# Dilated queries and keys as 2x2 block products: seven products for eight, in a written order

## The chip, the cores and the metric

The kernel runs on one core of one Trainium2 chip. A core has a matrix engine (PE; its weight loads are listed apart, as PEld), three engines for elementwise work (DVE, ACT, POOL), a queue that issues the DMAs (SP) and 16 DMA engines. SBUF holds the working data, PSUM (8 banks of 128 x 512 float32) takes the results of PE. Every engine runs its own instructions in order; semaphores join them. The metric is the device time of one execution in microseconds; lower is better.

## What is computed

One layer of an encoder trunk over 1024 tokens of width 1024, all in float32:

```
h = rmsnorm(x, attn_norm_g)
proj = h @ w_in                      # 1024 x 8096, cut into
# c_q 256 | c_kv 128 | k_rope 32 | z_mla 512 | q_dil 1536 | k_dil 1536 | v_dil 1536 | z_dil 512 | g_mla, g_dil 1024 each
a_out = mla_attention(c_q, c_kv, k_rope, ...)          # 8 heads, dense
d_out = dilated_mixture(q_dil, k_dil, v_dil, positions) # 3 groups of 8 heads of 64
y_mla = (a_out * silu(z_mla)) @ w_o_mla
y_dil = (d_out * silu(z_dil)) @ w_o_dil
merged = sigmoid(g_mla + b) * y_mla + sigmoid(g_dil + b') * y_dil
out = rmsnorm(x + merged @ w_out, final_norm_g)

def dilated_mixture(q, k, v, positions):
    q, k = rope(q heads, positions), rope(k heads, positions)
    for g, (window, dilation) in enumerate(((128, 1), (512, 4), (2048, 16))):
        o, lse = dilated_group(q[g], k[g], v[g], dilation, window // (2 * dilation))
    return sum over g of softmax(lse over g) * o
```

The change is in `q_dil` and `k_dil`: h (1024 x 1024) times 3072 columns of `w_in`, then the rotation by position.

## The kernel before

A float32 product is made of three: each operand is split into a high part `h` (rounded to the matrix engine's fp32r format) and a low part `l`, and `mm3` (line 67) adds h*h, h*l and l*h in one PSUM bank. `split` (line 73) writes the high part with ACT and the low part with the engine it is given. A `w_h`, `w_l` or `hT_h`, `hT_l` in the profile is such a pair.

The stages, in order of the program:

1. `latent_proj` reads x transposed (`xt`), scales it by the norm's gain and keeps it split in SBUF as `hTh`, `hTl` (8 pieces of 128 features x 1024 tokens). The factor of each token (the norm's rsqrt) is applied later, as `R` or `rcol`. `tables` makes cosines and sines, `latents` the queries, keys and values of the dense attention, `dil_v` (line 335) the dilated values, in six calls of 256 columns. Products go to the pool `pj_a` of six PSUM banks; `latents` has a pool of two (`pj_l`).
2. `dil_qk` (line 371) runs twelve times: two halves of the heads (`quad`) x three groups x q and k. One run, an "item", loads two weight tiles of 1024 x 128 (`wtile`, line 79): the first halves of four heads and their second halves, so that the rotation mixes the two results elementwise. For each half of the tokens (512) it makes the two products (`proj_half`: 8 pieces x 3 matmuls each), then `rope` (line 227): four products on DVE, read from PSUM, and two sums on POOL. The result is split (groups 0 and 1; ACT and POOL) or copied (group 2; ACT) into `dq_st`, group 1 and 2 in the order of their dilation, and after both halves it is stored per head to the tensors `s_dq`, `s_dk` in DRAM (line 404).
3. `dil_attention` goes over four pairs of heads and three groups. `dil_head` (line 610) loads q, k and v of one head into `op_b`, `op_a`, `op_c` and works in four steps: scores into `s_ps` (line 634), mask and maximum on DVE with the table `masks` (`soft_block`), exp on ACT, transposes (642), products with v (655, 663). `dil_classes` does group 2. PE's waits are filled by `fillers`: the projections of z and of the gates, pulled a few matmuls at a time by `feed`, one PSUM bank (`pj_b`); nineteen steps of three matmuls (`FIRST_FEED`) stand ahead of the attention.
4. `mla_attention` and then `output`.

The order of the instructions on each engine is not written out: a scheduler goes through the program with a model of the times and issues what is ready, earlier program lines first. Tiles live in pools stacked from the left and the right end of SBUF; a tile of a later pool waits until the tiles that had its place are done. All DMAs are issued by SP (line 65).

Of the kernel before, what the change touches and what calls it, by code (L numbers as in the profile page):

```python
# [39 lines left out]


# [8 lines left out]
class Net:  # L50
# [16 lines left out]
    def mm3(self, out, lh, ll, rh, rl, start, stop):  # L67
        mm = self.nc.tensor.matmul
        mm(out, lh, rh, start=start, stop=False)  # L69
        mm(out, lh, rl, start=False, stop=False)  # L70
        return mm(out, ll, rh, start=False, stop=stop)  # L71
# [7 lines left out]
    def wtile(self, src, wp=None, n=8):  # L79
        raw = self.wp.tile([128, 8, 128], F32, name="w_raw")  # L80
        wp = wp or self.wp
        h = wp.tile([128, 8, 128], F32R, name="w_h")
        l = wp.tile([128, 8, 128], F32R, name="w_l")
# [4 lines left out]
    def proj_half(self, w, half, pool):  # L88

        return run_all(self.proj_steps(w, half, pool))  # L90

    def proj_steps(self, w, half, pool):
# [3 lines left out]
        for kc in range(8):  # L96
            self.mm3(ps, w[0][:, kc], w[1][:, kc], self.hTh[:, kc, t], self.hTl[:, kc, t], kc == 0, kc == 7)
            if kc < 7:
                yield
# [235 lines left out]
    def dil_v(self, g, quad, tp, pj):  # L335
# [3 lines left out]
        for kk in range(2):  # L339
            raw = self.wp.tile([128, 4, 256], F32, name="w_raw")  # L340
            wp = (self.wp, self.wpx)[kk]
            h = wp.tile([128, 4, 256], F32R, name="w_h")
            l = wp.tile([128, 4, 256], F32R, name="w_l")
            self.dma(raw, a["wv"][g * 2 + quad, kk])
            self.split(raw, h, l, nc.gpsimd)
            w.append((h, l))
        for t in range(8):
            ps = pj.tile([128, 512], F32, name="pj")[:, :256]
            for kc in range(8):
                wh, wl = w[kc // 4]  # L350
                sl = slice(128 * t, 128 * t + 128)
                self.mm3(ps, self.hTh[:, kc, sl], self.hTl[:, kc, sl], wh[:, kc % 4], wl[:, kc % 4], kc == 0, kc == 7)
# [18 lines left out]
    def dil_qk(self, g, quad, which, tp, pj):  # L371

        nc, a = self.nc, self.a
        base = T_QK + (g * 2 + quad) * 4 + which * 2
        wa, wb = self.wtile(a["wt"][base]), self.wtile(a["wt"][base + 1], wp=self.wpx)
        if g < 2:
            st = [[tp.tile([128, S], F32R, name=f"dq_st{c}{p}") for p in range(2)] for c in range(2)]
        else:
            st = [[tp.tile([128, S], F32, name=f"dq_st{c}0")] for c in range(2)]
        for half in range(2):  # L380
            c512 = slice(half * 512, half * 512 + 512)
            pa, pb = self.proj_half(wa, half, pj), self.proj_half(wb, half, pj)
            o = self.rope(pa, pb, self.cos_d[:, c512], self.sin_d[:, c512], tp)
            for c in range(2):
                if g == 0:
                    self.split(o[c], st[c][0][:, c512], st[c][1][:, c512], nc.gpsimd)
                    continue
                if g == 1:
                    src = o[c].rearrange("p (m r) -> p r m", r=4)
                    dst = [x.rearrange("p (r m) -> p r m", r=4)[:, :, 128 * half:128 * half + 128] for x in st[c]]  # L390
                    self.split(src, dst[0], dst[1], nc.gpsimd)
                else:

                    src = o[c].rearrange("p (m b e) -> p e b m", b=8, e=2)
                    dst = st[c][0].rearrange("p (e b m) -> p e b m", e=2, b=8)[:, :, :, 32 * half:32 * half + 32]
                    for e in range(2):
                        nc.scalar.copy(out=dst[:, e], in_=src[:, e])
        off = 64 if (g == 0 and which) else 0
        dst = (self.dq if which == 0 else self.dk)[g]
        for c in range(2):  # L400
# [619 lines left out]
```

## Time and profile before

| | us |
|---|---|
| runs of the kernel before | 1333.44, 1323.28, 1328.5; median 1328.5 |
| the profiled execution | 1329.38 |
| its span, first to last instruction | 1327.2 |
| mean granted PE clock | 0.983 |

The profile is one execution. A row of a group gives the line, engine, operation, what it writes and reads, shapes and count, then busy time, mean ns of one, and the idle time of the engine ahead of it with what ended it. A row of a timeline begins with start and duration in us. A row of windows gives busy time (and instructions) of PE, PEld, DVE, ACT and POOL in a stretch of the span, then the granted clock of PE, the share of the DMA engines and GB/s. `L69`, `L70`, `L71` are the three matmuls of `mm3`, wherever it is called from. Starts of matmuls are measured and their ends are modelled, so the distance of starts is what one costs.

The span in 40 slices of 33.2 us (digits are tenths of a slice):

```profile
PE   8999999999999999988989899999999999999998
DVE  7463520222222224656576565656555566559622
ACT  6533332223322335545455463455554555444322
POOL 2251212676467644525422040312111022135522
PEclk9899999999999999989999999999999999999999
```

The stage of `dil_qk` is the stretch of slices 8 to 15 in which DVE shows 2.

### The profile page before, as it was taken

What the parts mean: (1) busy time and instruction counts of PE and PEld (TensorE: products, weight loads), DVE (VectorE), ACT (ScalarE), POOL (GpSimd) and SP (SyncE); (2) the same over time, 40 slices, a digit from 0 to 9 for tenths busy, and PEclk for the clock granted to TensorE, in tenths of its full rate; (3) what the DMA queues carried; (4) which work ended last, traced back from release to release, by engine and by line L of the source; (5) the groups of instructions that cost most, each with busy time, mean ns of one, the idle gap of its engine ahead of it and who ended that gap; (6) DMA issues with size and microseconds to landing.
All of it is one profiled execution on the core that took longest, in us unless ns stands there. A gap on an engine that the chain in (4) does not pass through costs nothing.

```text
span 1327.2 us, 19295 instructions
## 1 busy us (share of the span) xinstructions
PE 1272.2 (96%) x7101; PEld 1106.5 (83%) x7101; DVE 647.8 (49%) x1204; ACT 563.5 (42%) x1102; POOL 455.3 (34%) x302
## 2 busy tenths in 40 slices
PE   8999999999999999988989899999999999999998
PEld 8898999888888887877878777788888888887786
DVE  7463520222222224656576565656555566559622
ACT  6533332223322335545455463455554555444322
POOL 2251212676467644525422040312111022135522
PEclk9899999999999999989999999999999999999999
DMA  9757563575345435678777788636333463136322
GB/s 321 225 163 295 194 238 111 144 212 153 112 110 155 134 111 155 159 188 223 192 186 209 200 211 189 173 106 160 95 92 108 104 178 121 61 123 210 128 93 77
DMA packets 128254, 213.04 MB, mean 161 GB/s; under 512 B 36440, under 2 KB 65696, under 8 KB 126304
## 3 DMA queue, kind: packets, MB, share of 16 engines
q1 hardware_dynamic: 128160, 211.81, 55.2%
q8 instruction: 56, 0.92, 0.3%
q14 instruction: 38, 0.31, 0.1%
HBM read 143.01 MB, written 68.75 MB: 160 GB/s over the span
## 4 chain that ended last, share of the span: by engine, by line
PE 69%; DMA 9%; DVE 6%; issue 2%; SPq 1%; ACT 1%; POOL 0%; DVEq 0%; ACTq 0%; POOLq 0%
PE pj L69 17%; PE pj L71 16%; PE pj L70 16%; PE pt L543 4%; PE av L551 2%; PE av L552 2%; PE s_mla L69 2%; PE s_mla L70 2%; PE s_mla L71 2%; DMA s_sd<-av_t 2%; PE pt L642 1%; PE av L663 1%; SPq L65 1%; PE s_ps L698 1%; PE s_ps L634 1%
## 5 line engine op out<-in xcount | busy, mean ns | idle before, releaser
L76 POOL TENSOR_TENSOR w_l<-w_raw,w_h 128x1024 fp32r<-128x1024 f32 (+1 forms) x70 | 167.5, 2396 | 440.3 <-ACT w_h L75 390.3
L69 PE MATMUL pj<-hT_h,w_h 128*128 128x512 f32 x768 | 314.5, 410 | 2.2 <-DVE zg_z L428 2.1
L71 PE MATMUL pj<-hT_h,w_l 128*128 128x512 f32 x768 | 301.9, 393 | 0.0
L70 PE MATMUL pj<-hT_l,w_h 128*128 128x512 f32 x768 | 301.2, 392 | 0.0
L233 DVE TENSOR_TENSOR rope_m<-pj,cs_d 128x512 f32<-128x512 f32 x96 | 61.8, 686 | 241.1 <-PE pj L71 236.5
L76 DVE TENSOR_TENSOR pt_l<-pt,pt_h 128x512 fp32r<-128x512 f32 x192 | 131.4, 686 | 91.5 <-ACT pt_h L75 89.4
L71 PEld LDWEIGHTS pj<-hT_h,w_l 128*128 128x128 f32 x768 | 145.0, 189 | 31.6
L69 PEld LDWEIGHTS pj<-hT_h,w_h 128*128 128x128 f32 x768 | 145.5, 189 | 27.6 <-DVE zg_z L428 3.0
L75 ACT CAST pt_h<-pt 128x512 fp32r<-128x512 f32 x192 | 112.0, 584 | 130.3 <-PE pt L543 62.1
L70 PEld LDWEIGHTS pj<-hT_l,w_h 128*128 128x128 f32 x768 | 145.8, 190 | 24.6
L70 PE MATMUL pj<-w_l,hT_h 128*128 128x256 f32 x384 | 109.1, 284 | 0.0
L71 PE MATMUL pj<-w_h,hT_l 128*128 128x256 f32 x384 | 108.9, 284 | 0.0
L69 PE MATMUL pj<-w_h,hT_h 128*128 128x256 f32 x384 | 108.9, 284 | 0.0
L75 ACT CAST w_h<-w_raw 128x1024 fp32r<-128x1024 f32 (+1 forms) x70 | 72.3, 1034 | 73.9 <-PE pj L70 59.4
L529 DVE TENSOR_REDUCE m_nm<-s_mla 128x1 f32<-128x1024 f32 x64 | 78.0, 1220 | 33.2 <-PE s_mla L71 33.1
L608 ACT ACTIVATE p<-p,d_st 128x256 f32<-128x256 f32 x128 | 64.4, 504 | 58.5 <-DVE d_st L607 58.5
L532 ACT ACTIVATE p<-s_mla,m_nm 128x1024 f32<-128x1024 f32 x64 | 71.8, 1122 | 25.4 <-PE pt L543 18.4
L543 PE MATMUL pt<-consts,p 128*128 128x128 f32 x512 | 79.7, 276 | 1.8 <-ACT p L532 1.8
L69 PEld LDWEIGHTS pj<-w_h,hT_h 128*128 128x128 f32 x384 | 73.7, 192 | 1.1
L70 PEld LDWEIGHTS pj<-w_l,hT_h 128*128 128x128 f32 x384 | 73.7, 192 | 0.8
L71 PEld LDWEIGHTS pj<-w_h,hT_l 128*128 128x128 f32 x384 | 73.5, 191 | 0.7
L607 DVE CUSTOM_DVE_ANT_0 p<-s_ps,masks 128x256 f32<-128x256 f32 x128 | 51.1, 417 | 45.9 <-PE s_ps L635 25.2
(232 smaller groups left out, 2532.6 us busy)
## 6 DMA issues: line engine op xcount, KB each, us to landing
w_raw<-wt SPq DMA_DIRECT2D x48, 512.0 KB, 4.4
op_b<-s_dq SPq DMA_DIRECT2D x32, 512.0 KB, 8.6
s_dq<-dq_st SPq DMA_DIRECT2D x80, 128.0 KB, 2.5
s_dk<-dq_st SPq DMA_DIRECT2D x80, 128.0 KB, 2.6
gate<-s_gt SPq DMA_DIRECT2D x34, 256.0 KB, 3.0
s_dv<-dv_st SPq DMA_DIRECT2D x32, 256.0 KB, 4.7
s_gt<-zg_t SPq DMA_DIRECT2D x32, 256.0 KB, 4.0
w_raw<-wv SPq DMA_DIRECT2D x12, 512.0 KB, 6.3
```

What stands on the lines that cost most here:

```text
L69: mm(out, lh, rh, start=start, stop=False)
L70: mm(out, lh, rl, start=False, stop=False)
L71: return mm(out, ll, rh, start=False, stop=stop)
L75: self.nc.scalar.copy(out=h, in_=raw)
L76: sub.tensor_tensor(out=l, in0=raw, in1=h.bitcast(F32), op=ALU.subtract)
L233: v.tensor_tensor(out=mi, in0=p, in1=tab, op=ALU.mult)
L529: v.tensor_reduce(out=nm[:, hh, qb:qb + 1], in_=s, axis=AX.X, op=ALU.max, negate=True)
L532: nc.scalar.activation(out=p, in_=s, func=AF.Exp, bias=nm[:, hh, qb:qb + 1], accum_out=den[:, hh, qb:qb + 1])
L543: self.anchor = nc.tensor.transpose(pt[:, o:o + 128], P[b2][:, 128 * kc:128 * kc + 128], self.ident)
L551: nc.tensor.matmul(a_out, vv[:, kc], ph[:, s], start=kc == 0, stop=False)
L607: nc.vector.tensor_tensor_reduce(out=p, in0=s, in1=mask, op0=ALU.add, op1=ALU.min, scale=-0.125, scalar=3e38, accum_out=nm)
L608: nc.scalar.activation(out=p, in_=p, func=AF.Exp, scale=-1.0, bias=nm, accum_out=den)
```

## The change

The product of one item, 512 x 2 tokens by 1024 features by 128 x 2 columns, is seen as 2x2 blocks: activations X[i, k] (token half i, feature half k) and weights B[k, j] (feature half k, tile j). Instead of eight block products it makes seven (the Winograd form of Strassen's scheme): sums of the activation blocks are made once, differences of the weight blocks once an item, and the products are combined in PSUM and on DVE.

- `block_sums`: reads `xt` a second time and leaves four sums in split form, `s0` to `s3` (128 x 4 x 512, high and low, 64 KB a partition together). ACT scales, POOL sums, ACT and DVE split. It stands in the source behind the first two `dil_v` calls.
- `block_loads`, `block_minus`, `block_operand`: the two weight tiles of an item come as raw float32; POOL makes four differences in place; each of the seven operands (128 x 4 x 128) is split by ACT and POOL, five products ahead (`LEAD`).
- `block_product`: 4 pieces x 3 matmuls into one of the banks a, b, c, d; the fifth to seventh add to a, c, d. Two sets of four banks take turns.
- `block_steps`: what follows a product, each step at a place counted in products. ACT copies a and c out while they are partial (`st_c`); DVE adds these to the other banks, in PSUM; the rotation is done on DVE, cosines and sums in place in PSUM; ACT writes the high parts, DVE the low parts, and stores follow per half of the tokens.
- `blocks`: the loop over places, inside `manual_schedule`: there each engine issues the region's instructions in the order of the source. Instructions from outside may still be put between them by the scheduler.
- Weight tiles elsewhere (`wtile`, `dil_v`) are split in pieces of half the size, with twice the buffers. The pool of `dil_v`'s staging lies at the right end now; zeros and tables stand elsewhere in the source, the zeros are made by POOL.
- `s_dq`, `s_dk` keep high and low part side by side (`8, 2, 32, parts, S`). Group 1 keeps the two token halves apart, so `dil_head` reads its keys of a class as two runs of 128; k is loaded with one DMA for each part.

```diff
+LEAD = 5
...
-    def wtile(self, src, wp=None, n=8):
+    def wtile(self, src, wp=None, n=8, bufs=4):
...
-        self.split(raw[:, :n], h[:, :n], l[:, :n], self.nc.gpsimd)
-        return h, l
+        for k in range(0, n, 4):
+            m = min(4, n - k)
+            h = wp.tile([128, 4, 128], F32R, name="w_h", bufs=bufs)
+            l = wp.tile([128, 4, 128], F32R, name="w_l", bufs=bufs)
+            self.split(raw[:, k:k + m], h[:, :m], l[:, :m], self.nc.gpsimd)
+            w.append((h, l))
+        return w
...
+    def block_sums(self, sp, tp):
...
+        self.sh = [sp.tile([128, 4, 512], F32R, name=f"s{i}_h") for i in range(4)]
+        self.sl = [sp.tile([128, 4, 512], F32R, name=f"s{i}_l") for i in range(4)]
+        for kc in range(4):
+            y = {}
+            for i in range(2):
+                for k in range(2):
+                    x = y[i, k] = tp.tile([128, 512], F32, name=f"y{i}{k}", bufs=2)
+                    c = kc + 4 * k
+                    self.dma(x, a["xt"][i, :, c])
+                    nc.scalar.mul(x, x, self.ga[:, c:c + 1])
+            p.tensor_tensor(out=y[1, 1], in0=y[1, 0], in1=y[1, 1], op=ALU.add)
+            p.tensor_tensor(out=y[1, 0], in0=y[0, 0], in1=y[1, 0], op=ALU.subtract)
+            p.tensor_tensor(out=y[0, 0], in0=y[1, 1], in1=y[0, 0], op=ALU.subtract)
+            p.tensor_tensor(out=y[0, 1], in0=y[0, 1], in1=y[0, 0], op=ALU.subtract)
+            for i, x in enumerate((y[1, 1], y[0, 0], y[1, 0], y[0, 1])):
+                self.split(x, self.sh[i][:, kc], self.sl[i][:, kc], nc.vector)
+
+    def block_loads(self, n, item):
+
+        raw = [self.raw_pools[n % 2].tile([128, 8, 128], F32, name="w_raw", bufs=2) for _ in range(2)]
+        for i in range(2):
+            self.dma(raw[i], self.a["wt"][item[0] + i])
+        self.blk[n] = {(k, i): raw[i][:, 4 * k:4 * k + 4] for k in range(2) for i in range(2)}
+
+    def block_minus(self, j, items):
+
+        n, k = divmod(j, 7)
+        if n < len(items) and k in (2, 3, 4, 6):
...
+            self.nc.gpsimd.tensor_tensor(out=b[out], in0=b[x], in1=b[y], op=ALU.subtract)
+
+    def block_operand(self, j, items):
+
+        n, k = divmod(j, 7)
+        if n < len(items):
+            wp = (self.wp, self.wpx)[j % 2]
+            h = wp.tile([128, 4, 128], F32R, name="w_h", bufs=4)
+            l = wp.tile([128, 4, 128], F32R, name="w_l", bufs=4)
+            self.split(self.blk[n][((0, 0), (1, 0), (0, 0), (0, 1), (0, 0), (1, 1), (1, 0))[k]], h, l, self.nc.gpsimd)
+            self.opd[j] = h, l
+
+    def block_product(self, j, ps):
+
+        k = j % 7
+        hx = lambda i, c: tuple(x[:, 4 * c:4 * c + 4, 512 * i:512 * i + 512] for x in (self.hTh, self.hTl))
+        act = (lambda: hx(0, 0), lambda: hx(0, 1), lambda: self.s[0], lambda: self.s[2], lambda: self.s[1], lambda: self.s[3], lambda: hx(1, 1))[k]()
+        w = self.opd.pop(j)
+        out = ps["abcdacd"[k]]
+        for kc in range(4):
+            self.mm3(out, w[0][:, kc], w[1][:, kc], act[0][:, kc], act[1][:, kc], k < 4 and kc == 0, k in (1, 4, 5, 6) and kc == 3, skip=True)
+
+    def block_steps(self, n, item, ps, tp):
...
+        def copied(i, x):
+            tmp[i] = tp.tile([128, 512], F32, name="st_c", bufs=2)
+            act.copy(out=tmp[i], in_=x)
+        def both():
+            tmp["t"] = tp.tile([128, 512], F32, name="st_t")
+            v.tensor_tensor(out=tmp["t"], in0=d, in1=tmp[1], op=ALU.add)
+        add = lambda x, i: v.tensor_tensor(out=x, in0=x, in1=tmp[i], op=ALU.add)
+        steps = {
+            2: [lambda: copied(0, a)],
+            3: [lambda: add(b, 0)],
+            4: [lambda: copied(1, c)],
+            5: [both],
+            6: [lambda: copied(2, a), lambda: add(a, "t")],
+            7: [lambda: add(c, 2)],
+            9: [lambda: add(d, 2)],
+        }
...
+        r0, r1 = rope(0, b, c), rope(1, d, a)
+        put(7, r0[0])
+        put(8, r0[1])
+        put(8, r0[2])
+        put(9, r1[0])
+        put(10, lambda: high(0, (b, c)))
+        put(10, r1[1])
+        put(11, r1[2])
+        put(11, lambda: low(0, (b, c)))
+        put(12, lambda: high(1, (d, a)))
+        put(12, lambda: store(0))
+        put(12, lambda: low(1, (d, a)))
+        put(13, lambda: store(1))
+        return steps
+
+    def blocks(self, items, tp, pp):
...
+        for n in range(2):
+            self.block_loads(n, items[n])
+        for j in range(LEAD):
+            self.block_minus(j, items)
+            self.block_operand(j, items)
+        self.block_minus(LEAD, items)
+        with self.tc.manual_schedule():
+            for x in range(1, places + 14):
+                n, k = divmod(x - 1, 7)
+                j = x - 1
+                if j < places:
...
+                    self.block_product(j, ps[n])
+                todo = []
+                for m, y in ((n, k + 1), (n - 1, k + 8)):
+                    if m in steps:
+                        todo += steps[m].pop(y, [])
+                for f in todo:
+                    f()
+                self.block_operand(j + LEAD, items)
+                self.block_minus(j + LEAD + 1, items)
+                if k == 2 and n + 2 < len(items):
+                    self.block_loads(n + 2, items[n + 2])
...
-        self.dma(k[:, :S + pad], self.dk[g][h].rearrange("a c r t -> (a c r) t"))
+        for p in range(2):
+            self.dma(k[64 * p:64 * p + 64, :S + pad], self.dk[g][h].rearrange("c r p t -> p (c r) t")[p])
...
+                    self.dil_v(0, 0, vp, pj)
+                    self.dil_v(0, 1, vp, pj)
+                    sp = sums.enter_context(tc.tile_pool(name="sums", reuse_waits="tile", bufs=1))
+                    with tc.tile_pool(name="bs", reuse_waits="tile", bufs=1) as tp:
+                        self.block_sums(sp, tp)
+                        self.dil_v(1, 0, vp, pj)
+                    for g, quad in ((1, 1), (2, 0), (2, 1)):
+                        self.dil_v(g, quad, vp, pj)
...
+                with tc.tile_pool(name="dt", reuse_waits="tile", bufs=1, side="right") as tp, tc.tile_pool(name="st", reuse_waits="tile", bufs=1, space=PSUM) as pp:
+                    self.blocks([(T_QK + (g * 2 + quad) * 4 + which * 2, g, quad, which) for quad in range(2) for g in range(3) for which in range(2)], tp, pp)
```

The three closures of `rope` in `block_steps` are two products with the sine into `rope_m`, two with the cosine in place, and the sum and difference in place; `high` and `low` are the two parts of `split`; `store` issues one DMA for each head and row half, in group 2 only after the second token half.

More of the change, by code (lines that the diff above doesn't have):

```diff
@@ L340, in dil_v @@
             raw = self.wp.tile([128, 4, 256], F32, name="w_raw")
-            wp = (self.wp, self.wpx)[kk]
-            h = wp.tile([128, 4, 256], F32R, name="w_h")
-            l = wp.tile([128, 4, 256], F32R, name="w_l")
             self.dma(raw, a["wv"][g * 2 + quad, kk])
-            self.split(raw, h, l, nc.gpsimd)
-            w.append((h, l))
+            for k in range(0, 4, 2):
+                wp = (self.wp, self.wpx)[kk]
+                h = wp.tile([128, 2, 256], F32R, name="w_h", bufs=4)
+                l = wp.tile([128, 2, 256], F32R, name="w_l", bufs=4)
+                self.split(raw[:, k:k + 2], h, l, nc.gpsimd)
+                w.append((h, l))
         for t in range(8):
@@ L369, in dil_v @@
                 self.dma(self.dv[2][128 * t:128 * t + 128, quad * 256:quad * 256 + 256], st.rearrange("p h d -> p (h d)"))
-    def dil_qk(self, g, quad, which, tp, pj):
+    def block_sums(self, sp, tp):
         nc, a = self.nc, self.a
[L374 to L380, printed above, removed]
-            c512 = slice(half * 512, half * 512 + 512)
[L382 to L400, printed above, removed]
-            for p in range(len(st[c])):
-                for j in range(4):
-                    self.dma(dst[quad * 4 + j, p, c, :, off:off + S], st[c][p][32 * j:32 * j + 32])
@@ L491, in o_proj @@
         for j in js:
[L492 removed]
+            wh, wl = self.at(w3, dt) if j == 3 and w3 else self.at(w, w0 + j)
             self.mm3(ps, wh, wl, br[0][:, j, c], br[1][:, j, c], j == js[0], j == js[-1])
@@ new lines, in run @@
+                    for g, quad in ((1, 1), (2, 0), (2, 1)):
+                        self.dil_v(g, quad, vp, pj)
+                    for x in (self.cos_d, self.sin_d):
+                        for half in range(2):
+                            c = slice(512 * half, 512 * half + 512)
+                            nc.gpsimd.tensor_tensor(out=x[:, c], in0=x[:, c], in1=self.R[:, c], op=ALU.mult)
+                    z = vp.tile([128, 8, 64], F32, name="zero", bufs=1)
+                    nc.gpsimd.memset(z, 0.0)
```

134 lines of the change are left out of this document (93 added, 41 removed).

## The prediction

> **What bounds the kernel now.** I read the page first, then windows around the stage that is changed, then the timeline at its edges, the waits and the groups by form. The page says who is busy:
>
> ```profile
> span 1327.2 us, 19295 instructions
> PE 1272.2 (96%) x7101; PEld 1106.5 (83%) x7101; DVE 647.8 (49%) x1204; ACT 563.5 (42%) x1102; POOL 455.3 (34%) x302
> ```
>
> PE is busy 96% of the span, but busy time is an average. The stage in question, the dilated q and k projections, is found by its edges on PE: the first row is its first matmul, the last three its end and the first matmul of the fillers behind it. Then come windows before, of and after the stage (columns: PE, PEld, DVE, ACT, POOL busy, granted clock, DMA share, GB/s).
>
> ```profile
> 225.69 0.40 PE L69 MATMUL pj<-hT_h,w_h 128*128 128x512 f32 x1
> ...
> 486.38 0.39 PE L70 MATMUL pj<-hT_l,w_h 128*128 128x512 f32 x1
> 486.61 0.39 PE L71 MATMUL pj<-hT_h,w_l 128*128 128x512 f32 x1
> 486.84 0.39 PE L69 MATMUL pj<-hT_h,w_h 128*128 128x512 f32 x1
> ...
> 184.70:225.70 41.00, 41.00 (x344) 41.00 (x344) 0.67 (x1) 10.00 (x18) 4.86 (x3) 1.00 0.36 124
> 225.70:486.80 261.10, 261.10 (x1154) 216.21 (x1153) 60.54 (x94) 69.11 (x84) 159.76 (x102) 1.00 0.51 142
> 486.80:500.30 13.50, 12.20 (x58) 9.88 (x57) 2.41 (x5) 4.27 (x7) 5.89 (x6) 1.00 0.55 169
> ```
>
> The stage is 12 items x 2 weight tiles x 2 halves x 8 pieces x 3 = 1152 matmuls. From 225.69 to 486.84 are 261.15 us, so they start 0.2267 us apart; the 0.39 of a row is latency. PE is never idle there at granted clock 1.00, while DVE and ACT are a quarter busy and POOL 61%. Here a matmul left out is worth 0.2267 us, until another engine becomes the bound. Times are made against the profiled execution, 1329.38 us around its span of 1327.2, and that lies 0.9 over the median of the runs, 1328.5.
>
> **The saving.** Seven products of 4 pieces x 3 matmuls replace 96 matmuls by 84 an item: 12 x 12 x 0.2267 = 32.6 us. A product takes 12 x 0.2267 = 2.72 us, an item of seven 19.05, the stage 228.5. That holds only if the other engines keep up with 19.05 us an item. Their prices:
>
> ```profile
> L233 DVE TENSOR_TENSOR rope_m<-pj,cs_d 128x512 f32<-128x512 f32 x96 | 61.8, 686 | 241.1 <-PE pj L71 236.5 <-POOL rope_m L235 4.6
> L76 DVE TENSOR_TENSOR mg_l<-gate,m 128x512 fp32r<-128x512 f32 x16 | 20.0, 1258 | 1.5 <-ACT m L75 1.2
> L234 POOL TENSOR_TENSOR rope_m<-rope_m,rope_m 128x512 f32<-128x512 f32 x26 | 33.6, 1294 | 88.3 <-DVE rope_m L233 88.3
> L826 POOL TENSOR_TENSOR gate<-gate,m 128x512 f32<-128x512 f32 x16 | 24.9, 1574 | 19.4 <-DVE gate L825 19.4
> L432 POOL TENSOR_TENSOR zg_t<-zg_t,zg_z 128x512 f32<-128x512 f32 x16 | 20.7, 1294 | 1.3
> L75 ACT CAST pt_h<-pt 128x512 fp32r<-128x512 f32 x192 | 112.0, 584 | 130.3 <-PE pt L543 62.1 <-PE av L551 32.6 <-PE pt L642 24.3
> L75 ACT CAST dq_st<-rope_m 128x512 fp32r<-128x512 f32 x9 | 9.6, 1066 | 23.6 <-POOL rope_m L234 9.2 <-POOL rope_m L235 8.0 <-DMA s_dq<-dq_st 6.1
> L75 ACT CAST m<-gate 128x512 fp32r<-128x512 f32 x16 | 9.9, 620 | 12.4 <-POOL gate L826 12.4
> 242.01 1.06 ACT L75 CAST w_h<-w_raw 128x1024 fp32r<-128x1024 f32 x1 [1.23 <-PE pj L70]
> 243.14 2.39 POOL L76 TENSOR_TENSOR w_l<-w_raw,w_h 128x1024 fp32r<-128x1024 f32 x1 [0.52 <-ACT w_h L75]
> ```
>
> DVE, an item: 5 sums of products, 4 sines, 4 cosines, 4 rotary sums, 4 low parts (not in group 2) = 21 operations of 128x512. All have one operand in PSUM and one in SBUF, as the row of 686 ns: 21 x 0.686 = 14.4 us. Twelve write back into PSUM, which no row does. The ends are 0.645 (two back to back take 1.29 in the timeline row further below) and 1.258, the dearest row; I take 0.686, since only the place of the output differs. At 1.258 the item is 12 x 1.258 + 9 x 0.686 = 21.3, 2.2 over, +27 us in all.
>
> ACT: 3 copies out of PSUM at 0.584, 7 casts of weights at 0.620, 4 high parts at 1.066 in group 1 (strided) and less elsewhere: 10.4 us. Hidden behind PE.
>
> POOL loses the rotary sums and the low parts and gets 7 low parts of weights and 4 differences of weight blocks: 11 x 1.294 = 14.2 us, before 159.8/12 = 13.3. But POOL and ACT now wait for each other in a written order: a difference, the cast of it, its low part, and only then the next difference. Cast to low part costs a hop of 0.07 (242.01 + 1.06 to 243.14), taken twice: 4 x (1.294 + 0.620 + 0.14 + 1.294) + 3 x 1.294 = 17.3 of 19.05. Tight, but five products of lead (13.6 us) absorb a burst. So no stall; bounds 0 and, with every POOL operation at 1.574, 20.4 an item, +16 us. Behind a late cast ACT's copies of the first product's bank are queued, and PE's fifth product waits for these; two products, 5.4 us, lie between. If DVE or POOL lost this cover, PE would pay the item's excess twelve times.
>
> DMA: loads of 2 x 512 KB an item as before; stores are again 16 of 128 KB (8 in group 2), with runs of 2 KB for 4. The share was 0.51, each load is issued some 7 products ahead, each store buffer is refilled four or more places after its store. The cover is that lead: at 4 places it is 10.9 us, for 8 issues and a landing (rows in the last fence: 3.59 and 2.5, the load 4.4). Nothing; without it, up to 6.1 us once an item.
>
> **The start.** block_sums reads x again and makes four sums in split form: 16 loads, 16 products and 16 casts on ACT, 16 sums on POOL, 16 differences on DVE. Its buffers lie where the latents' were, so it starts when these are done:
>
> ```profile
> L76 DVE TENSOR_TENSOR mla_st<-pj,mla_st x16: 690/692/692, 111.9 to 184.7; 128x512 fp32r<-128x512 f32 x16
> x_t<-xt SPq DMA_DIRECT2D x16, 256.0 KB, 6.1
> L143 ACT ACTIVATE hT_h<-x_t,consts 128x512 fp32r<-128x512 f32 x16 | 11.2, 720 | 4.1 <-DMA x_t<-xt 3.9
> L917 POOL TENSOR_TENSOR cs_d<-cs_d,R x4: 1297/1373/1616, 72.4 to 76.6; 128x512 f32<-128x512 f32 x4
> ```
>
> 184.7 + 0.7 + 6.1 + 0.7 = 192.2 for POOL's first sum. Sixteen take 20.7 us (25.2 at 1.574), the first four low parts and three differences of item 0 another 9.1: done at 222 to 226.5, and last cast and difference 2 us on. The cover is the rest of the dilated values: 41 us of PE with POOL busy 4.86 and DVE 0.67. Products 0 and 1 need no sums, so the limit is 225.7 + 5.4 = 231.1: met. The tables times R, moved in the source, run at 72.4 when ready, and the zeros likewise: nothing. Splitting weights in halves adds instructions, no bytes; in the windows above PE waits for no weight: nothing. The eight banks replace six plus two; PE may wait for the last eviction: 0 to 0.6, I take 0.5.
>
> DVE has two SBUF operands only in these 16 differences. The rows show what that does beside POOL: mg_l at 1258 next to gate at 1574, where POOL's rope_m, beside DVE work that reads PSUM, stays at 1294, as does zg_t among the attention's DVE work. The Trainium skill, "SBUF — State Buffer", section "SBUF: two separate sides", says that a VectorE operation with two SBUF inputs and a GpSimd operation hold their port pair exclusively, each for its whole instruction. The pair of slow rows agrees with that. It speaks for the first rival below and, by its other half, against a slower POOL inside the stage, where DVE reads one operand from PSUM.
>
> **The end.** Before, the first head's operands came early and PE went from fillers to scores:
>
> ```profile
> L65 SPq DMA_DIRECT2D op_b<-s_dq x48: 573/604/2325, 261.1 to 795.1; - x48
> 490.41 3.59 SPq L65 DMA_DIRECT2D s_dk<-dq_st  x8
> 492.28 0.28 PE L634 MATMUL s_ps<-op_a,op_b 128*128 128x256 f32 x1
> 492.40 0.28 PE L635 MATMUL s_ps<-op_a,op_b 128*128 128x256 f32 x1
> 494.10 0.37 SPq L65 DMA_DIRECT2D masks<-masks  x1
> 499.77 0.42 DVE L607 CUSTOM_DVE_ANT_0 p<-s_ps,masks 128x256 f32<-128x256 f32 x1 [6.60 <-DMA s_zs<-zg_t]
> 500.26 0.39 PE L634 MATMUL s_ps<-op_a,op_b 128*128 128x256 f32 x1 [1.30 <-DVE d_st L607]
> op_a<-s_dk SPq DMA_DIRECT2D x8, 512.0 KB, 11.0
> s_dq<-dq_st SPq DMA_DIRECT2D x80, 128.0 KB, 2.5
> w_raw<-wt SPq DMA_DIRECT2D x48, 512.0 KB, 4.4
> 236.80 1.29 DVE L233 TENSOR_TENSOR rope_m<-pj,cs_d 128x512 f32<-128x512 f32 x2 [4.15 <-PE pj L71]
> PE s_ps L634 <- DMA op_b<-s_dq: 4.6, 1, 4.6
> PE s_ps L634 <- DMA op_a<-s_dk: 2.5, 1, 2.5
> ```
>
> Now the sums fill the place of those buffers up to the last item's products 2 to 5, so the loads start 10.9 to 2.7 us before the stage's end and land, at 11.0, some 0 to 8 us after it. After the last product DVE still has 11 operations, 7.5 us, ACT four copies more, 10.1; then SP issues 8 stores (3.59). PE's cover is the first feed, 19 steps x 3 x 0.2267 = 12.9 us, and 8 scores of 0.12 (492.28 to 492.40): 13.9. The masks need a buffer of the stage: with the end of DVE's part at 7.5 and 5.7 from issue to use (494.10 to 499.77), DVE begins near 13.2; before, it began 499.77 - 486.84 = 12.9 after the stage. So about equal. Bounds: -1.3 (the idle row goes) and +13, when the loads queue behind the stores: 13.7 + 5 issues of 0.6 + 11 = 27.7 against 13.9. I take 1.5, near the equal case. Late next would be DVE's soft_block, and scores behind it.
>
> In attention, k comes in two DMAs for one: 16 issues of some 0.6 on SP, 9.3 us, hidden by loads issued a head ahead; the waits for operands, 4.6 + 2.5, bound a gain. Nothing. Group 1's keys move as two runs of 128; the group-0 products of probabilities and values (L655) already move such runs, at no higher price than the plain ones of group 1 (L663):
>
> ```profile
> L655 PE MATMUL av<-pt_h,op_c 128*128 128x256 f32 x80 | 20.9, 284 | 0.0
> L663 PE MATMUL av<-pt_h,op_c 128*128 128x256 f32 x64 | 16.9, 291 | 0.0
> ```
>
> **The sum.** 1329.4 - 32.6 + 0.5 + 1.5 + 1 for hops inside the stage (between 0 and the 16 above) = 1299.8; less the 0.9 to the median, 1299.
>
> **Rivals.**
> - The sums come late. If DVE's differences and POOL's sums exclude each other, a pair costs 1.294 + 0.686 = 1.98, sixteen 31.7; 192.2 + 31.7 + 9.1 + 2 = 235, 4 past 231.1. For it: gate and mg_l. Against: POOL's slack before 225. 1303. By the skill's port rule this is the case. Chance 0.15.
> - POOL and ACT's chain binds: at 1.574 the stage is 12 x 20.4 = 244, 1315. For it: only gate; against: zg_t at 1294 beside a busy DVE. 0.10.
> - Attention starts late, by 13: 1311. For it: SP is one queue in order, and the prefetch from 261.1 is gone. Against: loads become ready before the last stores do. 0.10.
> - Slower: DVE's writes back to PSUM. The item is 12y + 6.2; the time passes +1% when the stage is 11 us longer than before, 22.7 an item, y = 1.38, and 1343. Against: every row is below. 0.05.
> - The gain is handed back, attention waiting on something off this path: 1327. Against: PE bound on both sides. 0.04.
>
> **How the numbers follow.** The forecast has 0.56. About 1%, 13 us, is what a measurement of this kernel can tell from no change: 1315 is the border. Faster: 0.55 of the forecast, 0.14, 0.04, 0.08 of the first three rivals = 0.81. Same: 0.05 + 0.02 + 0.04 + 0.02 = 0.13. Slower 0.06. The range reaches down to 1290 (idle of 1.3 and operand waits of 7.1 gone) and up to 1317, over the first three rivals; left out are half of the second, the last two and a little below: 0.17.
>
> **What would show it.** Right: 1008 matmuls 0.2267 apart from near 226, the last near 455, PE without waits there; DVE near 75% busy, its PSUM-writing rows near 686, POOL's near 1294. A wait of the third product of item 0 on a sum means the first rival; waits of every fifth or sixth product on ACT's copies, the second; idle PE before the first scores, the third; DVE rows above 1.1 us, the fourth. The prediction is wrong if PE waits inside the stage at a steady beat, or if attention grows by more than 10 us.

## The result, and the profile after

The changed kernel takes 1320.66 us (median of 20 runs, 1314.72 to 1330.69); the kernel before took 1328.13 (median of 20 runs beside it, one of which took 2083.65). The ratio is 0.9945, with a 95% interval of 0.9929 to 0.9960: some 7 us faster, where 29.5 were forecast, and outside the range of 1290 to 1317. The profiled execution is 1320.48 us around a span of 1318.6, 8.6 less than before. Windows of the changed kernel show where the rest went: the stage, from its end to the scores for which PE waits on DVE's first masked sum (scores plus mask, with their maximum), and from there to the end (columns as in the prediction).

```profile
226.24:460.93 234.69, 234.69 (x1008) 190.51 (x1009) 144.70 (x230) 93.34 (x179) 166.93 (x131) 0.99 0.58 147
460.93:487.68 26.75, 12.30 (x58) 9.70 (x56) 7.13 (x15) 5.05 (x12) 4.32 (x5) 0.85 0.90 216
487.68:1318.60 830.92, 792.28 (x4396) 680.66 (x4396) 482.10 (x895) 401.81 (x865) 238.23 (x192) 0.97 0.54 149
```

Each edge is set beside that of before (225.69, 486.84, 500.26, 1327.2):

| | before | after | difference | forecast |
|---|---|---|---|---|
| start of the stage | 225.69 | 226.24 | +0.55 | +0.5 |
| the stage | 261.15 | 234.69 | -26.46 | -31.6 (-32.6, +1 for hops) |
| its end to the scores behind the first masked sum | 13.42 | 26.75 | +13.33 | +1.5 |
| from there to the end | 826.94 | 830.92 | +3.98 | 0 |
| span | 1327.2 | 1318.6 | -8.6 | |

The matmuls went, 1008 for 1152, and with them 32.6 us. 24.0 of these came back: 13.3 behind the stage, 6.1 inside it, 4.0 later and 0.6 ahead of it.

**The end.** PE's largest new wait is that for DVE's masked sum: 15.6 us in four waits, the longest 13.3.

The timeline behind the stage shows what DVE waits for (start, duration, engine, line, out<-in, and in brackets the idle time ahead and what ended it; SPq is SP's queue):

```profile
458.60 3.22 SPq L67 DMA_DIRECT2D op_b<-s_dq  x2
...
465.74 4.77 SPq L67 DMA_DIRECT2D w_raw<-wt  x1
...
470.61 10.40 SPq L67 DMA_DIRECT2D s_dk<-dq_st  x8
...
483.24 0.36 SPq L67 DMA_DIRECT2D masks<-masks  x1
483.29 0.42 POOL L1114 MEMSET pt_h<- 128x384 f32 x1 [23.16 <-DMA s_dk<-dq_st]
...
487.19 0.42 DVE L777 CUSTOM_DVE_ANT_0 p<-s_ps,masks 128x256 f32<-128x256 f32 x1 [19.62 <-DMA masks<-masks]
...
487.68 0.58 PE L808 MATMUL s_ps<-op_a,op_b 128*128 128x256 f32 x1 [13.27 <-DVE d_st L777]
```

Loads for two heads (the burst, below) and a load of filler weights stand in SP's queue ahead of the last eight stores. With the DMA engines at a share of 0.9, the weights take 4.77 us to issue and the stores 10.4, for 3.59 before. The masks are issued only when the stores have landed, as their place in SBUF is that of the tiles that the stores read. DVE sits at the first masked sum for 19.6 us. Behind it in DVE's queue stands the next eviction of the filler's bank (the read that frees a PSUM bank), so PE has nothing left: its last 24 filler matmuls end near 474.

**The stage.** These rows are the first matmuls of products 0, 1, 2, 3 and 6 of item 2 and of the item behind it:

```profile
266.80 0.39 PE L71 MATMUL st_a<-hT_h,w_h 128*128 128x512 f32 x1
...
269.52 0.39 PE L71 MATMUL st_b<-hT_h,w_h 128*128 128x512 f32 x1
...
272.24 0.40 PE L71 MATMUL st_c<-s_h,w_h 128*128 128x512 f32 x1
...
275.05 0.39 PE L71 MATMUL st_d<-s_h,w_h 128*128 128x512 f32 x1
...
283.45 0.40 PE L71 MATMUL st_d<-hT_h,w_h 128*128 128x512 f32 x1
...
286.21 0.39 PE L71 MATMUL st_a<-hT_h,w_h 128*128 128x512 f32 x1
```

A product on hT takes 2.72 us (266.80 to 269.52), one on a tile of sums 2.80 or 2.81, product 6 behind them 2.76. PE waits for nothing in between, and the clock granted in this item is 1.00. The item is 19.41 us for 19.05: 12 x 0.37 = 4.4 us.

**The start.** PE's last projection started at 222.66; then:

```profile
206.99 1.74 POOL L398 TENSOR_TENSOR y<-y,y 128x512 f32<-128x512 f32 x1
...
225.19 0.62 ACT L77 CAST s_h<-y 128x512 fp32r<-128x512 f32 x1 [3.60 <-POOL y L398]
225.72 0.47 ACT L376 ACTIVATE dv_s<-pj,rcol 128x256 f32<-128x256 f32 x1
...
226.24 0.50 PE L71 MATMUL st_a<-hT_h,w_h 128*128 128x512 f32 x1 [3.29 <-ACT dv_s L376]
```

POOL's sums take up to 1.74 us and end late. ACT has a cast of a sum (225.19) ahead of the eviction of the dilated values (225.72) that the stage's bank needs, and PE idles 3.29 us. Then the first product of item 0 runs at half the pace for a while: its 12 matmuls take 4.45 us for 2.72.

### The profile page after: what moved, and what is told of

The parts are those of the page before. It is cut to its first block, busy times and chain, and to the rows that moved or that the text cites. A ratio compares the mean times of both kernels' runs of the same rounds, so it can differ in the third digit from the quotient of the medians.

```text
span 1318.6 us, 19629 instructions
## 1 busy us (share of the span) xinstructions
PE 1249.8 (95%) x6957; PEld 1082.7 (82%) x6957; DVE 750.9 (57%) x1359; ACT 610.4 (46%) x1276; POOL 499.5 (38%) x393
## 4 chain that ended last, share of the span: by engine, by line
PE 65%; DMA 14%; DVE 5%; issue 3%; POOL 2%; SPq 2%; ACT 1%; DVEq 0%; ACTq 0%; POOLq 0%
PE pj L71 9%; PE pj L72 9%; PE pj L73 9%; PE pt L713 4%; DMA s_sd<-av_t 3%; DMA op_a<-s_dk 3%; PE av L722 2%; PE av L721 2%; PE s_mla L71 2%; SPq L67 2%; PE s_mla L73 2%; PE s_mla L72 2%; PE st_a L71 2%; PE st_a L73 2%; PE st_a L72 2%
## 5 line engine op out<-in xcount | busy, mean ns | idle before, releaser
L78 POOL TENSOR_TENSOR w_l<-w_raw,w_h 128x512 fp32r<-128x512 f32 (+1 forms) x176 | 232.6, 1330 | 452.5 <-ACT w_h L77 383.4
L71 PE MATMUL pj<-hT_h,w_h 128*128 128x512 f32 x384 | 167.0, 435 | 1.8 <-DVE zg_z L598 1.8
L72 PE MATMUL pj<-hT_l,w_h 128*128 128x512 f32 x384 | 153.7, 400 | 0.0
L73 PE MATMUL pj<-hT_h,w_l 128*128 128x512 f32 x384 | 153.7, 400 | 0.0
L77 ACT CAST w_h<-w_raw 128x512 fp32r<-128x512 f32 (+1 forms) x176 | 106.1, 614 | 100.8 <-POOL w_raw L415 65.0
L73 PEld LDWEIGHTS pj<-hT_h,w_l 128*128 128x128 f32 x384 | 74.1, 193 | 16.6
L71 PEld LDWEIGHTS pj<-hT_h,w_h 128*128 128x128 f32 x384 | 75.0, 195 | 12.5 <-DVE zg_z L598 2.5
L72 PEld LDWEIGHTS pj<-hT_l,w_h 128*128 128x128 f32 x384 | 75.1, 196 | 10.0
L721 PE MATMUL av<-pt_h,op_c 128*128 128x256 f32 x256 | 69.0, 289 | 1.4 <-ACT pt_h L77 1.4
```

The source lines that it names most:

```text
L71: mm(out, lh, rh, start=start, stop=False, skip_group_check=skip)
L72: mm(out, lh, rl, start=False, stop=False, skip_group_check=skip)
L73: return mm(out, ll, rh, start=False, stop=stop, skip_group_check=skip)
L77: self.nc.scalar.copy(out=h, in_=raw)
L78: sub.tensor_tensor(out=l, in0=raw, in1=h.bitcast(F32), op=ALU.subtract)
L721: nc.tensor.matmul(a_out, vv[:, kc], ph[:, s], start=kc == 0, stop=False)
```

## The experiments

Ratios are to the kernel before, run beside it on the same chip; the changed kernel has 0.9945.

**The masks' place.** The store tiles get a pool of their own at the lower end of the stage's buffers:

```diff
-                    st[i, half] = tp.tile([128, 2, 512], F32R, name=f"dq_st{i}{half}")
+                    st[i, half] = sq.tile([128, 2, 512], F32R, name=f"dq_st{i}{half}")
```

> The tiles that the stores read (dq_st) move to the lower end of the stage's buffers, so that the masks come to lie where weights of item 11 lay, which are free long before the stores; nothing else changes, the loads of two heads' operands still go out ahead of the last stores. Theory 1 (the shared place holds the masks back): they are issued ahead of the last eight stores, the first masked sum starts about when DVE is through with the stage, the idle 13.3 us ahead of the first scores falls to 3 or less, and with it the slow clock behind it goes (2.5): 1305 to 1311 us against 1320.7. Theory 2 (the burst holds everything back): the masks queue behind six loads of 512 KB, the DMA engines stay full to about 479, idle of 5 to 10 stays: 1313 to 1318. The eight stores should still take about 10 us to issue by both.

Measured: 0.9911 (0.9886 to 0.9936).

```profile
469.65 2.39 SPq L67 DMA_DIRECT2D masks<-masks  x1
...
481.76 0.42 DVE L777 CUSTOM_DVE_ANT_0 p<-s_ps,masks 128x256 f32<-128x256 f32 x1 [15.42 <-DMA masks<-masks]
482.25 0.58 PE L808 MATMUL s_ps<-op_a,op_b 128*128 128x256 f32 x1 [9.10 <-DVE d_st L777]
```

The masks now go ahead of the stores, 13.6 us earlier, and take 12.1 us to their use, for 4.0 in the changed kernel (483.24 to 487.19). The idle falls only from 13.3 to 9.1: the second theory, the place having a smaller part. That part is read from the trace; the ratio alone does not show it, as padding (below) has 0.9920.

**The sums' engine.** Two of the four sums of each row go to DVE:

```diff
-            p.tensor_tensor(out=y[1, 1], in0=y[1, 0], in1=y[1, 1], op=ALU.add)
-            p.tensor_tensor(out=y[1, 0], in0=y[0, 0], in1=y[1, 0], op=ALU.subtract)
+            nc.vector.tensor_tensor(out=y[1, 1], in0=y[1, 0], in1=y[1, 1], op=ALU.add)
+            nc.vector.tensor_tensor(out=y[1, 0], in0=y[0, 0], in1=y[1, 0], op=ALU.subtract)
```

> Eight of the sixteen sums of activations go from POOL to DVE. Theory 1 (POOL, at 1.74 us an operation beside DVE's differences, ends its sums last and holds ACT's queue and with it the last eviction of dilated values): the sums end 8 us or more earlier, PE's 3.3 us of idle ahead of the stage and the slow first product behind it (4.45 for 2.72) go: 1315 to 1317 us against 1320.7. Theory 2 (ACT is late there for other reasons, or the first product is slow for another reason than the idle): 1319 to 1321, with the idle or the 4.45 still there.

Measured: 0.9884 (0.9857 to 0.9912). The idle ahead of the stage falls to 1.77 us, still behind ACT's eviction, and the first product takes 2.85 us; the stage ends 3.0 us earlier (457.94 for 460.93). The first theory, in part. The ratio fell by more than these 3 us, and nothing in the trace accounts for the rest: the profiled execution took 1320.18 us and lost 2.8 of the 3.0 again behind the first masked sum.

**32 bytes of padding.**

```diff
+        nc.vector.memset(sp.tile([128, 8], F32, name="pad"), 0.0)
         self.sh = [sp.tile([128, 4, 512], F32R, name=f"s{i}_h") for i in range(4)]
```

> 32 bytes of padding (and one memset of 32 bytes) ahead of the eight tiles of sums, so that they begin at the same offset within 64 bytes as hT and the weights do. Theory 1 (that offset sets the cadence): the products of sums go from 0.2334 to 0.2267 us a matmul, an item from 19.41 to 19.05, the stage 3.8 to 4.4 us shorter: about 1316.5 us against 1320.7. Theory 2 (the values, the place in the SBUF or the accumulation onto a used bank set it): 0.2334 stays, 1320.7.

Measured: 0.9920 (0.9903 to 0.9937); products 2 to 5 still take 2.79 to 2.81 us. The first theory falls. The ratio is 0.0025 under that of the changed kernel although no product became shorter, so a difference of this size between two groups of runs says little.

**More cover.**

```diff
-FIRST_FEED = 19
+FIRST_FEED = 40
```

> The first feed is 40 steps of filler matmuls for 19, 21 x 3 x 0.2267 = 14.3 us more of work between the stage and the first scores. Theory 1 (PE only lacks work there, and attention has steps to spare): the idle 13.3 and the slow clock behind it go, 1305 to 1309 us. Theory 2 (the steps taken forward are missing as cover later in the attention): the idle goes at 460.9 to 487.7 and comes back as waits of transposes, scores or projections: 1316 to 1321.

Measured: 1.0106 (1.0085 to 1.0128), slower than before by 1%, and no test of either theory: behind the stage PE does what it did, the same 24 filler matmuls and 12.48 us of idle ahead of the scores behind the masked sum. The fillers have one bank. Its eviction stands behind the masked sum in DVE's queue, so a longer feed in the source puts no work ahead of it; what its order costs later, 1.6% against the changed kernel, I did not follow.

**The second head's loads.** Here only the place of three loads in SP's queue changes:

```diff
+        with self.tc.issue_after(self.mask_load.ins) if g == 0 and h in (1,) else ExitStack():
+            for rows in (slice(0, 64), slice(64, 128)):
+                self.dma(q[rows], self.dq[g][h].rearrange("c r p t -> (c r) p t"))
...
-                    self.dma(m, self.a["masks"])
+                    self.mask_load = nc.sync.dma_start(out=m, in_=self.a["masks"])
```

> As the changed kernel, with the masks where they were, but the second head's three operands are loaded behind the masks in SP's queue instead of ahead of the last stores: 1.6 MB less in the burst. Theory 1 (the stores, and the masks behind them, wait for the bytes of the burst): at some 200 GB/s that is 8 us, the eight stores issue in 4 to 6 us instead of 10.4, the masks 6 to 9 us earlier, idle ahead of the scores 5 to 7 us for 13.3: ratio to the kernel before about 0.989 (the changed kernel 0.9945). Theory 2 (the masks wait for the place alone, until the stores have landed, whatever is queued): idle stays 11 to 13, ratio 0.993 to 0.996; a wait for the second head's operands, later, may eat what is won by either.

Measured: 0.9862 (0.9839 to 0.9884).

```profile
467.43 3.59 SPq L67 DMA_DIRECT2D s_dk<-dq_st  x8
473.05 0.35 SPq L1110 DMA_DIRECT2D masks<-masks  x1
...
478.23 0.39 PE L809 MATMUL s_ps<-op_a,op_b 128*128 128x256 f32 x1 [3.47 <-DVE d_st L777]
```

The stores are back at 3.59 us, the masks 10.2 us earlier, the idle is 3.47 us: first theory. Without these loads ahead of the stores 9.8 of the 13.3 us are gone (the loads are 2 x 512, 2 x 288 and 576 KB, 2.2 MB and not the 1.6 of the expectation), and waits of 0.8 and 1.6 us for operands follow.

**Other operands.** What makes a product on the sums slow? The main line of the edit; POOL's four sums are left out besides, and product 4 takes its rows from the four tiles:

```diff
-        act = (lambda: hx(0, 0), lambda: hx(0, 1), lambda: self.s[0], lambda: self.s[2], lambda: self.s[1], lambda: self.s[3], lambda: hx(1, 1))[k]()
+        act = (lambda: hx(0, 0), lambda: hx(0, 1), lambda: hx(1, 0), lambda: self.s[2], lambda: self.s[1], lambda: (hx(1, 0)[0], self.s[3][1]), lambda: hx(1, 1))[k]()
```

> The products' operands are exchanged and POOL's sums of activations left out, so the output is another: product 2 of each item reads a block of hT, product 3 a tile of sums that holds a plain block of x, product 4 such tiles a row from each of four (8 KB apart for 2 KB), product 5 the high part of hT and the low part of a sums' tile. Theory 1 (values): products 3 and 4 go to 0.2267 us a matmul. Theory 2 (the place of the tiles, in the lower half of the SBUF): 3 and 4 stay at 0.2334, 2 goes to 0.2267, 5 in between. Theory 3 (the place in the order, accumulation on a bank in use): 2 and 5 stay at 0.2334 too. At the start, without POOL's sums: if POOL beside DVE was the cause, DVE's differences fall from 1478 ns to 700 to 900, and PE's 3.3 us of idle ahead of the stage goes.

Measured, in one execution, by the first matmuls of products 2, 3, 5 and 6 of one item:

```profile
267.66 0.39 PE L71 MATMUL st_c<-hT_h,w_h 128*128 128x512 f32 x1
...
270.38 0.40 PE L71 MATMUL st_d<-s_h,w_h 128*128 128x512 f32 x1
...
275.99 0.40 PE L71 MATMUL st_c<-hT_h,w_h 128*128 128x512 f32 x1
...
278.77 0.40 PE L71 MATMUL st_d<-hT_h,w_h 128*128 128x512 f32 x1
```

On hT product 2 takes 2.72 us; products 3 and 4, plain values in the sums' tiles, 5.61; the mixture 2.78. So neither the values nor the place in the order make the price: it goes with the tile that is read. PE no longer idles ahead of the stage. DVE's differences fall to 1140 ns, not to 700 to 900: 690 where POOL does nothing, more where it splits weights.

**Both edits of the end.** The first and fifth runs' edits together.

> Both edits of the end together: the masks' place is that of weights of item 11 (as in the first run) and the second head's loads go behind the masks and the last stores. Theory 1 (burst and place each hold a part of the 13.3 us): the masks are issued near 466, land by 473, the idle ahead of the scores is 2 us or less, and the slow clock goes: ratio to the kernel before 0.982 to 0.986. Theory 2 (something else is late next, the first head's operands or the second head's): idle of 4 or more at the scores or a new wait near 490, ratio 0.987 to 0.991.

Measured: 0.9845 (0.9825 to 0.9866). The masks are issued at 459.07, PE no longer waits for the first masked sum, and what is late next is the second head:

```profile
480.54 0.35 PE L809 MATMUL s_ps<-op_a,op_b 128*128 128x256 f32 x1 [4.07 <-DMA op_a<-s_dk]
```

So both theories hold: the ratio is the first's, the new wait the second's. The interval overlaps that of the loads alone.

**All sums on DVE as well.**

```diff
-        p = nc.gpsimd
+        p = nc.vector
```

> As the run before, and all sixteen sums of activations on DVE, none on POOL. If the start's loss (3.3 us of idle, 1.7 of slow clock) was POOL beside DVE, it goes too: DVE's 32 operations take about 22 to 26 us from 190, the first product starts within 0.5 us of the last projection, and the ratio is 0.978 to 0.983, some 1302 us. If DVE with twice the work is late itself, PE waits for a sum at the third product of item 0 and nothing is won.

Measured: 0.9826 (0.9799 to 0.9852), 1308.83 us against 1334.07. This version is faster than the kernel before, by 1.5 to 2%, and its interval lies below that of the changed kernel. Its sums, then its windows of the stage and of the stretch behind it:

```profile
203.06 0.69 DVE L78 TENSOR_TENSOR s_l<-y,s_h 128x512 fp32r<-128x512 f32 x1
...
206.58 1.78 DVE L78 TENSOR_TENSOR s_l<-y,s_h 128x512 fp32r<-128x512 f32 x1
207.78 1.74 POOL L78 TENSOR_TENSOR w_l<-w_raw,w_h 128x512 fp32r<-128x512 f32 x1
208.29 1.79 DVE L397 TENSOR_TENSOR y<-y,y 128x512 f32<-128x512 f32 x1
...
224.29 0.40 PE L71 MATMUL st_a<-hT_h,w_h 128*128 128x512 f32 x1
```

```profile
224.29:457.27 232.98, 232.98 (x1010) 189.21 (x1009) 140.88 (x227) 91.53 (x176) 164.00 (x129) 1.00 0.60 149
457.27:467.70 10.43, 9.25 (x45) 7.49 (x44) 6.64 (x12) 4.41 (x10) 2.43 (x4) 1.00 1.03 307
```

The stage begins with no idle time (no bracket behind its first matmul) and is 12 x 19.41 long, with no slow first product; the first masked sum comes 10.43 us behind it, for 26.26 (460.93 to 487.19). The rows of DVE and POOL between 206 and 210 start in turn, a pair every 1.71 us (206.58 to 208.29; POOL's next starts at 209.49), while either alone takes 0.69 and 1.29.

**Tiles on the other side.** Products 3 and 5 read tiles in pools on the right side, where hT and the weights lie; the sums are on the left, with the pools opened without a side:

```diff
+        act = (lambda: hx(0, 0), lambda: hx(0, 1), lambda: self.s[0], lambda: self.probe[0], lambda: self.s[1], lambda: self.probe[1], lambda: hx(1, 1))[k]()
...
+        x = [p.tile([128, 512], F32R, name="probe", bufs=1) for p in (self.dpool, self.wpx)]
+        for t in x:
+            self.nc.scalar.copy(out=t, in_=self.R[:, 0:512])
+        self.probe = [[[t] * 4] * 2 for t in x]
```

> Products 3 and 5 of each item read, as both parts and in all rows, one 2 KB tile on the right side of the SBUF instead of a tile of sums on the left: product 3 one at the upper end of the tables' pool, product 5 one at the upper end of the second weights' pool, just below R and hT; so the output is another. Products 2 and 4 read sums as before. Theory 1 (the side, or how low the tile lies): 2 and 4 stay at 0.2334 us a matmul, and 5, next to hT, goes to 0.2267; 3 shows on which side of the border the tables' place is. Theory 2 (it is hT alone, its size or its rows 4 KB apart): 3 and 5 stay at 0.2334.

Measured, in one execution:

```profile
268.89 0.40 PE L71 MATMUL st_c<-s_h,w_h 128*128 128x512 f32 x1
...
271.70 0.40 PE L71 MATMUL st_d<-probe,w_h 128*128 128x512 f32 x1
...
274.46 0.40 PE L71 MATMUL st_a<-s_h,w_h 128*128 128x512 f32 x1
...
277.28 0.40 PE L71 MATMUL st_c<-probe,w_h 128*128 128x512 f32 x1
...
280.04 0.39 PE L71 MATMUL st_d<-hT_h,w_h 128*128 128x512 f32 x1
...
282.76 0.39 PE L71 MATMUL st_a<-hT_h,w_h 128*128 128x512 f32 x1
```

Products on the sums take 2.81 and 2.82 us, on both probes 2.76, and product 6, behind a probe, 2.72 where it took 2.76 behind sums. Within a probe's product the first eight matmuls are still some 0.232 apart and the last four 0.227: as if something of the slow product ahead remained. The second theory falls: it is not hT alone. In this stage tiles on the right are read faster than the sums on the left, at the places tried. A probe on the left was not tried, so that one tile read again and again is fast on either side is not ruled out; where a border lies, and why, is open too.

**The last stores on ACT's queue.** The version with all edits, and:

```diff
-                        self.dma(dst[j, i, :, 0], st[i, 0][x])
+                        (self.dma if n < 11 else nc.scalar.dma_start)(dst[j, i, :, 0], st[i, 0][x])
```

> As the run with all sums on DVE, and the eight stores of the last item are issued from ACT's queue, so that SP can issue the second head's loads straight behind the masks instead of behind the stores: some 8 us earlier (from 460 for 468). Theory 1 (what is late next is the second head's operands, 3.6 us at 478): that wait falls under 1 us, ratio to the kernel before 0.979 to 0.982 where the run before had 0.9826. Theory 2 (the bytes are the same, the stores then land later or the masks share the engines with 1.6 MB): the masks' first use moves from 467.7 to 471 or later, and nothing is won: 0.982 to 0.985.

Measured: 0.9858 (0.9829 to 0.9887).

```profile
459.52 11.96 ACTq L524 DMA_DIRECT2D s_dk<-dq_st  x7
...
466.07 0.42 DVE L777 CUSTOM_DVE_ANT_0 p<-s_ps,masks 128x256 f32<-128x256 f32 x1 [6.46 <-DMA masks<-masks]
...
474.51 0.69 PE L817 MATMUL pt<-consts,p 128*128 128x128 f32 x2 [7.11 <-ACT p L778]
```

With the second head's loads in front again, seven stores hold ACT's queue for 11.96 us, and the exponentials stand behind them: PE waits 7.1 us for these instead of 3.6 for operands. The wait for operands is gone from there, as the first theory says, and nothing is won, as the second says, but by neither's mechanism: the masks' first use came at 466.07, earlier than 467.70 and not later. The burst held up ACT's queue as it had held up SP's. The interval overlaps that of the run with all sums on DVE, so a loss in time is not shown.

## Why the prediction was wrong, step by step

- **The start (+0.5; was +0.55).** Right by luck. POOL and DVE did hold each other up, as the first rival said, at 1.71 us a pair (the run with all sums on DVE) for that rival's 1.98. But no product waited for a sum. The cost came by ACT's queue: an eviction behind a cast of a late sum, 3.29 us of idle, hidden in the table because the last projection started at 222.66, for 225.57 before. The prediction named the last eviction, bounded it by 0.6, and did not ask what stands ahead of it in its queue. The Trainium skill, "SBUF — State Buffer", section "SBUF: two separate sides", has the loser of that port fully blocked; the alternating rows agree.
- **The slow first product (+1.7) was not in the sum.** After 3.29 us of idle item 0's first product took 4.45 us; after 1.77, in the run with two sums on DVE, 2.85; after none 2.72. The length of the idle time alone does not set it: in the run with both edits of the end 2.24 us cost as much, 4.45, and in the run with tiles on the other side 2.75 us cost next to nothing, 2.88. These are the first matmuls of products 0 and 1 of item 0, first in the one, then in the other:

```profile
224.41 0.50 PE L71 MATMUL st_a<-hT_h,w_h 128*128 128x512 f32 x1 [2.24 <-ACT dv_s L376]
...
228.86 0.39 PE L71 MATMUL st_b<-hT_h,w_h 128*128 128x512 f32 x1
```

```profile
224.68 0.50 PE L71 MATMUL st_a<-hT_h,w_h 128*128 128x512 f32 x1 [2.75 <-ACT dv_s L376]
...
227.56 0.39 PE L71 MATMUL st_b<-hT_h,w_h 128*128 128x512 f32 x1
```

  The Trainium skill, "TensorE: Matmul & The Clock Gate", section "Part 1: The HAM clock gate (the "warmup" mystery)", has the array fall to half its clock after an idle window of some 3.4 us. The half clock agrees (the slow matmuls stand 0.43 us apart for 0.2267, here and behind the 13.3 us of idle); the 3.4 does not, as 2.24 was enough.
- **The saving (-32.6; the stage gave -26.5).** The count was right, the price of 0.2267 a matmul was not: it was taken from rows that read hT. Four products of seven read tiles of sums at 0.2334, which is 4.4 us. With the 1.7 of the slow first product, and less the 1 for hops that did not occur, that makes the 5.1 between -31.6 and -26.46. The trace of before already had dearer matmuls of this shape: in its output stage 240 of them stand 0.2311 apart, without a wait and at granted clock 1.00.

```profile
1236.89 0.39 PE L70 MATMUL pj<-wout_l,m 128*128 128x512 f32 x1
...
1292.36 0.39 PE L70 MATMUL pj<-wout_l,m 128*128 128x512 f32 x1
```

- **DVE, ACT, POOL.** Right. The writes back to PSUM, taken at 0.686 between 0.645 and 1.258, measured 690 to 700; POOL's low parts of weights took 1305 for 1294:

```profile
L451 DVE TENSOR_TENSOR st_b<-st_b,st_c 128x512 f32<-128x512 f32 x12 | 8.4, 700 | 26.0 <-PE st_b L73 24.0 <-ACT dq_st L509 2.1
...
L487 DVE TENSOR_TENSOR st_c<-st_c,cs_d 128x512 f32<-128x512 f32 x12 | 8.3, 690 | 0.0
```

  PE waited for none of them inside the stage: the second and the fourth rival fell. DVE was busy 62% of the stage (144.70 of 234.69) for the 75% named as a sign: its rows follow each other 0.60 us apart (463.30, 463.90, 464.50), and four of the twelve items have no low parts.
- **The end (+1.5; was +13.3, and 4.0 behind it). This is the step that failed.** The prediction had the loads 0 to 8 us late, the stores issued in 3.59 us from their row of before, and the masks on time "with the end of DVE's part at 7.5". Both figures hold only if the burst does not lie ahead of the stores and if the masks need only DVE's tiles. It saw the upper bound, "+13, when the loads queue behind the stores", and had the order the wrong way round: the stores queue behind the loads, and the masks behind the stores. The third rival, 0.10, had the right size. Its counter-argument, that the loads become ready before the last stores do, was the mechanism. In the traces, moving the second head's loads removed 9.8 us of the 13.3; the place alone removed 4.2; both removed the wait for the masked sum altogether.
- **In attention (0; was +4.0).** Some 2.7 of it, by estimate, is the clock behind the idle (matmuls 0.43 apart from 487.7 to about 493). PE's waits for q and k of a head add up to 9.0 us (4.5 + 4.5), for the 7.1 that the prediction took as unchanged. No run changed this part alone, so that account is argued and not shown.
- **The sum.** With the start and the end mended the same products give 0.9826, some 1305 us on the forecast's scale, where 1299 were forecast. The price of reading the sums' tiles is 4.4, and the second head's operands, 3.6, are late next: PE's waits for q and k of a head come to 13.1 us there, for 7.1 before. The two are more than the 6 left, as the start and the end came out earlier than forecast (224.29 for 226.2, and a first masked sum 10.43 us behind the stage for 14.4).

## What to carry to other kernels

When a change takes the place of a prefetch, list what every queue will issue in the first microseconds after the stage, with its bytes, in order, and mark which of it another engine waits for first: here 2.2 MB that nobody needed yet stood ahead of the stores and of 0.6 MB of masks that everything needed. Look at whose memory the first small load of the next stage lies in. A cover of filler work counts only as far as its evictions do not queue behind the very wait that it should cover.

## What the hardware did that was not expected

In this stage a fp32r matmul of 128x512 starts every 0.2267 us when its moving operand (the tile of 512 columns) lies in hT, and every 0.2334 when it lies in the sums' tiles on the left: 3%, the same in every item, unchanged by 32 bytes of padding, by other values, or by rows 8 KB apart for 2. It was seen at granted clock 1.00, with no wait between the matmuls. Two tiles on the right, near hT, were read at the lower price after the first eight matmuls. This is no rule of two prices: the output stage of both kernels reads `wout`, whose pool is opened without a side like that of the sums, at 0.2311.
